# Where the bias of the exponentials is made, and the form of the rotary sums, in a two-layer hybrid attention trunk

## The chip, the cores and the metric

The kernel runs on one core of a Trainium2 chip. A core has TensorE (PE in the profile; PEld is its weight load), VectorE (DVE), ScalarE (ACT), GpSimd (POOL) and SyncE (SP), which here issues all DMAs. The metric is the device time of one execution in microseconds; the time given is the median of several runs.

## The reference

Two decoder layers over 1024 tokens of width 1024. Layer 0 uses mixer A, dilated sliding-window attention with 16 heads of 64 in three groups (window 128 with stride 1, 512 with stride 4, 2048 with stride 16), merged by their softmax denominators. Layer 1 uses mixer B, sliding-window attention (128) with 16 query heads on 2 key heads and one sink logit a head. Queries and keys are rotated; the output is gated by SiLU, projected, normed with a residual, and a second gate adds a projection of p.

```python
def apply_rope(t, cos, sin):
    t1, t2 = tf[..., :half], tf[..., half:]
    return jnp.concatenate([t1 * c - t2 * s, t2 * c + t1 * s], axis=-1)

# banded_attention, for each query over its band of keys
m = jnp.max(s, axis=-1, keepdims=True)
if sinks is not None:
    m = jnp.maximum(m, sk)
e = jnp.exp(s - m)
l = jnp.sum(e, axis=-1, keepdims=True)
if sinks is not None:
    l = l + jnp.exp(sk - m)
o = jnp.einsum('bnhgqk,bnkhd->bnqhgd', e, v) / l
...
for i in range(DEPTH):
    h = mixer(x)                       # A, then B
    x = layer_norm(DEEPNORM_ALPHA * x + h, ln_g[i], ln_b[i])
    x = x + sigmoid(x @ ple_w_gate[i]) * (p[i] @ ple_w_proj[i])
```

## The kernel before, in words

All large products run in float16 with operands split into a high and a low half (three matmuls for one, `lin`, lines 262 to 272). Weights come in blocks of 512 columns: SyncE loads a block, VectorE finds its largest value (line 108), ScalarE writes the high half (131) and VectorE the low half (132). A block's work is cut into eight token tiles of 128.

Layer A goes through two pairs of head quarters and in each through the three groups in the order 1, 2, 0; each group has its own token order (`token_orders`). For a group the values are made first (eight tiles), then two blocks of queries and keys. For each tile of these `rope_out` reads the product from PSUM: two multiplications on VectorE with the cosine and the sine (line 344, tiles t1 and t2), a difference and a sum on GpSimd over the 32-column halves (346, 347), then, one tile later, a split into high and low half (353, 354), a copy with halves exchanged (357) and a DMA transpose to qk (358).

A *unit* is the attention of four heads for one tile of queries: `scores` makes the scores on TensorE (381), masks them and takes the row maxima on VectorE (385), makes the bias nbias of the exponentials from the maxima, the negated scale ncs and a constant on VectorE (387), takes four exponentials on ScalarE (391), splits the result (395 on ScalarE, 397 on GpSimd or VectorE), and transposes it by DMA to pT (400). `pv` multiplies by the values, two units later in layer A and three in layer B. There are 96 units in layer A and 32 in layer B. The nbias columns are kept with the output in tile st in layer A (the merge of the groups reads them) and in tile sb in layer B.

In layer B the bias is also limited by the sinks: `self.nsink`, made once, holds the negated sink plus the constant, and line 389 takes the minimum on VectorE. For every second unit `after` makes the denominators of eight heads: the sum of bias and sinks (842, tile se), its exponential on ScalarE (843), the sum with the row sums (844) and the reciprocal (845). `outp` writes the scaled output to tile mu on VectorE (849).

The tables for rotation, in the three token orders, and the masks lie in one constant tile `tab`, loaded at the start in two pieces (452, 458).

The order of the instructions on each engine is set by the framework's scheduler, which simulates the program with its own costs: the code's order and waits are kept, but instructions of an engine can change places.

Of the kernel before, what the change touches and what calls it, by code (L numbers as in the profile page):

```python
# [10 lines left out]
F32 = mybir.dt.float32  # L11
# [3 lines left out]
AF = mybir.ActivationFunctionType  # L15
ALU = mybir.AluOpType
# [4 lines left out]
P = 128  # L21
S = 1024
D = 1024
NT = S // P
NK = D // P
PLE = 256
HD = 64
# [26 lines left out]
def const_table():  # L54
    inv = np.array(INV_FREQ, np.uint32).view(np.float32)
    ang = np.arange(S, dtype=np.float32)[:, None] * inv[None, :]
    cos = np.cos(ang.astype(np.float64)).astype(np.float32) * np.float32(2.0 ** -QK_SHIFT)
    sin = np.sin(ang.astype(np.float64)).astype(np.float32) * np.float32(2.0 ** -QK_SHIFT)
    rope = []
    for o in token_orders():  # L60
        for t in (cos, sin):
            rope.append(t[o].transpose(1, 0, 2).reshape(P, NT * 32))
    r = np.arange(P)[:, None]
    c = np.arange(P)[None, :]

    def m(keep):
        return np.where(keep, 0.0, NEG).astype(np.float32)

    parts = rope + [
        m(c >= r), m(c <= r),  # L70
        m(c >= r + 1), m(c <= r),
        m((c <= r) & ((c - r) % 2 == 0)),
        np.eye(P, dtype=np.float32),
    ]
    return np.ascontiguousarray(np.concatenate(parts, axis=1))
# [6 lines left out]
N_WAKE = 8  # L82
Z_AHEAD = 3
ROWS_AHEAD = 4
N_ROPE = 6 * NT * 32
N_CONST = N_ROPE + 6 * P


class Block:
# [49 lines left out]
class Trunk:  # L139
    def __init__(self, ctx, tc, a):  # L140
        self.ctx, self.tc, self.nc, self.a = ctx, tc, tc.nc, a
        nc = self.nc
# [25 lines left out]

        tab = self.const.tile([P, N_CONST], F32, name="tab")
        self.tab = tab  # L170
        self.cos, self.sin = [], []
        for o in range(3):
            for i, lst in enumerate((self.cos, self.sin)):
                b = (2 * o + i) * NT * 32
                lst.append(tab[:, b:b + NT * 32].rearrange("p (n c) -> p n c", n=NT))
        b = N_ROPE
        self.mask_a = tab[:, b:b + 2 * P]
        self.mask_b = tab[:, b + 2 * P:b + 4 * P]
        self.mask_2 = tab[:, b + 4 * P:b + 5 * P]
# [10 lines left out]
    def keep(self, cols=1, name="k"):  # L190
        self.uid += 1
        return self.const.tile([P, cols], F32, name=f"{name}{self.uid}", tag=f"{name}{self.uid}")

    def pow2(self, mx, s, inv):

# [134 lines left out]
        self.nc.vector.tensor_scalar(n, c, -1.0, None, op0=ALU.mult)  # L330
        return c, n

    def rope_out(self, ps, nq, nk, order, n, dst):

        nc, w = self.nc, self.work
        nh = nq + nk
        t1 = w.tile([P, 512], F32, tag="t1", name="t1")
        t2 = w.tile([P, 512], F32, tag="t2", name="t2")  # L340
        pv = ps.rearrange("p (h c) -> p h c", c=32)
        for t, tb in ((t1, self.cos[order]), (t2, self.sin[order])):
            tv = t[:, :nh * HD].rearrange("p (h c) -> p h c", c=32)
            nc.vector.tensor_mul(tv, pv, tb[:, n, :].unsqueeze(1).to_broadcast([P, 2 * nh, 32]))  # L344
        v1, v2 = (t[:, :nh * HD].rearrange("p (h b c) -> p h b c", b=2, c=32) for t in (t1, t2))
        nc.gpsimd.tensor_sub(v1[:, :, 0, :], v1[:, :, 0, :], v2[:, :, 1, :])  # L346
        nc.gpsimd.tensor_add(v1[:, :, 1, :], v1[:, :, 1, :], v2[:, :, 0, :])  # L347
        nb = nh + nk
        hl = w.tile([P, 12, P], F16, tag="hl", name="hl", bufs=3)
        rv = t1[:, :nh * HD].rearrange("p (h c) -> p h c", c=HD)  # L350

        def parts():
            nc.scalar.activation(hl[:, :nh, 0:HD], rv, AF.Copy)  # L353
            nc.gpsimd.tensor_sub(hl[:, :nh, HD:P], rv, hl[:, :nh, 0:HD])  # L354
            if nk:
                src, to = (hl[:, a:b, :].rearrange("p h (w c) -> p h w c", w=2) for a, b in ((nq, nh), (nh, nb)))
                nc.vector.tensor_copy(to, src[:, :, ::-1, :])  # L357
            nc.sync.dma_start(dst, hl[:, :nb, :].rearrange("p b c -> p (b c)"), transpose=True)

        self.ends.append(parts)  # L360
# [7 lines left out]
    def scores(self, qa, kas, mask, cs, ncs, sums, nbias, floor, pool_lo):  # L368
# [6 lines left out]
        for pr in range(2):  # L375
# [7 lines left out]
            for i in range(2):  # L383
                h = 2 * pr + i
                nc.vector.tensor_tensor_reduce(sm[:, h, :nk], ps[:, i, :nk], mask, 1.0, -3e38, ALU.add, ALU.max,  # L385
                                               mx[:, h:h + 1])
        nc.vector.tensor_scalar(nbias, mx, ncs, LN_PSCALE, op0=ALU.mult, op1=ALU.add)  # L387
        if floor is not None:
            nc.vector.tensor_tensor(nbias, nbias, floor, op=ALU.min)
        for h in range(4):  # L390
            nc.scalar.activation(sm[:, h, :nk], sm[:, h, :nk], AF.Exp, bias=nbias[:, h:h + 1], scale=cs,  # L391
                                 accum_out=sums[:, h:h + 1])
# [41 lines left out]
    def startup(self):  # L434
# [4 lines left out]
        with tc.tile_pool(name="start", bufs=1) as st:  # L439
# [9 lines left out]
                    nc.sync.dma_start(raw[:, 0, 1024 * kt:1024 * kt + n], a[src][0][:, 1024 * kt:1024 * kt + n])  # L449
            part(pr[:, 0, :], a["pT"][0], 256, 1024)  # L450
            part(wr[:, 0, :], a["wple"][0], 512, 1024)
            nc.sync.dma_start(self.tab[:, N_CONST - P:], a["tab"][:, N_CONST - P:])
            nc.sync.dma_start(pr[:, 1, :], a["pT"][1])
            nc.sync.dma_start(wr[:, 1, :], a["wple"][1])
            for c in range(NK):
                nc.sync.dma_start(xr[:, c, :], a["xT"][:, c, :])
            self.blocks[0].load()
            nc.sync.dma_start(self.tab[:, :N_CONST - P], a["tab"][:, :N_CONST - P])
            nc.sync.dma_start(self.sinks, a["sinks"].partition_broadcast(P))

            idle = st.tile([P, 512], F16, name="idle", tag="pro", bufs=14)
# [158 lines left out]
    def layer_a(self):  # L620
# [13 lines left out]
        cvs = {}  # L634
        for pair in range(2):
            for g in (1, 2, 0):
                blk = self.next_block()
                cvs[pair, g] = self.prod(self.invx, blk.inv, 2.0 ** V_SHIFT, "cv")
                slots = [i for i in range(3) if i != slots[1]]
# [7 lines left out]
                for i in range(2):  # L647
# [4 lines left out]
                    for n in range(NT):  # L652
                        ps = self.ps_lin.tile([P, 512], F32, tag="lin", name="lin")
                        self.lin(ps, blk, *self.stat_a(g, n), 0, 512)
                        qk.append(at.tile([P, 12, P], F16, tag="qk", name="qk", bufs=8))
                        self.rope_out(ps, 4, 4, g, n, qk[n])
                        self.unit_a(2 * pair + i, g, n, qk, v1, v2, cs, ncs,
                                    cvs[pair, g], scr)
                        self.progress()
# [122 lines left out]
    def layer_b(self, xT, invx):  # L782
# [2 lines left out]
        self.z_dr = [self.dram.tile([P, D], F32, name=f"zb{n}", tag=f"zb{n}") for n in range(NT)]  # L785
        self.set_lag(3)
        self.bufs = 3
        self.nsink = self.kv.tile([P, 16], F32, name="nsink", tag="nsink")
        nc.vector.tensor_scalar(self.nsink, self.sinks, -1.0, LN_PSCALE, op0=ALU.mult, op1=ALU.add)
        blk = self.next_block()  # L790
        cv = self.prod(invx, blk.inv, 2.0 ** V_SHIFT, "cv")
        ck = self.prod(invx, blk.inv, 2.0 ** QK_SHIFT, "ck")
# [3 lines left out]
        for n in range(NT):  # L796
            ps = self.ps_lin.tile([P, 512], F32, tag="lin", name="lin")
            self.lin(ps[:, :256], blk, *self.stat_t(xT, n), 0, 256)
            self.v_out(ps[:, P:2 * P].rearrange("p (h c) -> p h c", c=HD), vh[:, n], vl[:, n])
            self.rope_out(ps[:, :P], 0, 2, 0, n, kT[n])  # L800
            self.progress()
        blk.released = True
        self.upt = 1.5
        for kv in range(2):
# [3 lines left out]
            nc.vector.tensor_scalar(cs, cs, 1e-20, None, op0=ALU.max)  # L808
            ncs = self.keep(1, "ncs")
            nc.vector.tensor_scalar(ncs, cs, -1.0, None, op0=ALU.mult)  # L810
            for n in range(NT):
                ps = self.ps_lin.tile([P, 512], F32, tag="lin", name="lin")
                self.lin(ps, blk, *self.stat_t(xT, n), 0, 512)
                qT = at.tile([P, 8, P], F16, tag="qk", name="bq", bufs=9)
                self.rope_out(ps, 8, 0, 0, n, qT)
                tile_st = []
                for hg in range(2):
                    self.unit_b(kv, n, hg, qT, kT, vh, vl, cs, ncs, cv, tile_st)
# [5 lines left out]
    def unit_b(self, kv, n, hg, qT, kT, vh, vl, cs, ncs, cv, tile_st):  # L824
# [22 lines left out]
        def outp(o, r):  # L847
# [4 lines left out]

        self.later(UNIT_LAG, lambda: self.unit(lambda h: qT[:, 4 * hg + h, :], kas, mask, cs, ncs,
                                          lambda h, kb: vh[:, tiles[kb], kv, :], lambda h, kb: vl[:, tiles[kb], kv, :],
                                          stats, outp, hg == 1, self.nsink[:, c0:c0 + 4], after if hg else None))


    def transpose_rows(self, src, s, dst, i, name):
# [276 lines left out]
```

## Time and profile before

| | |
|---|---|
| median of 3 runs | 1719.22 us (1716.74 to 1722.72) |
| profiled execution | 1715.05 us, span 1713.3 us |
| mean granted TensorE clock | 0.980 |
| DMA | 309.06 MB, mean 180 GB/s |

All profile lines come from the one profiled execution. A row of instructions gives line, engine, operation, output<-input by the program's names, shapes and count, then the busy time in us and the mean ns of one, then the idle time of the engine before them and what ended it. A row with three numbers behind a colon, as 215/229/1759, gives the shortest, median and longest duration in ns. In the timeline the columns are start, length, engine, line and operation; the brackets at the end give the idle time before it and what ended it. A matmul's length includes its way through the pipeline, so matmuls that follow each other overlap: rows of 0.38 us start 0.22 us apart.

### The profile page before, as it was taken

Reading aid. Unit: us, or ns where it says so; the run is one execution under the profiler, and the core shown is the slowest. Engines: PE = TensorE matmul, PEld = TensorE weight load, DVE = VectorE, ACT = ScalarE, POOL = GpSimd, SP = SyncE. Lnnn points to the kernel's source line nnn. Section 1 sums busy time; section 2 is a strip of 40 time slices with the busy share of each in tenths; the row PEclk is TensorE's granted clock in tenths of the full one; section 3 lists DMA queues with packets and bytes.
Section 4 is the critical chain, followed back from the end, with each engine's and each line's share of the span. In section 5 each row is a group of like instructions: output and inputs, shape, how many; then the busy total and the mean of one; then the engine's idle time right before and its main releaser. Section 6 shows DMA issues by size and latency. Waiting matters only on the chain. (4 is left out here: it accounts for less than half of the span.)

```text
span 1713.3 us, 29175 instructions
## 1 busy us (share of the span) xinstructions
PE 1595.0 (93%) x10579; PEld 882.3 (51%) x10579; DVE 1163.1 (68%) x2846; ACT 837.6 (49%) x1818; POOL 700.2 (41%) x601
## 2 busy tenths in 40 slices
PE   9899999999998889999999988689999898979998
PEld 3455566654555456666545543234464555534444
DVE  6767656765677776567567776787457988767731
ACT  4425554554654365545545663523334677753221
POOL 1115524532655665155235553443324553123431
PEclk9999999999999999999999999799999999989999
DMA  9618865764778787477558887989965798787963
GB/s 367 225 59 163 161 142 128 161 142 117 154 155 220 184 165 153 112 155 162 120 131 169 182 221 224 297 226 259 251 172 113 143 188 179 170 277 217 239 201 111
DMA packets 542785, 309.06 MB, mean 180 GB/s; under 512 B 473008, under 2 KB 494128, under 8 KB 542256
## 3 DMA queue, kind: packets, MB, share of 16 engines
q1 hardware_dynamic: 542640, 307.20, 73.2%
q8 instruction: 83, 1.36, 0.3%
q14 instruction: 62, 0.51, 0.1%
HBM read 135.82 MB, written 54.92 MB: 111 GB/s over the span
## 5 line engine op out<-in xcount | busy, mean ns | idle before, releaser
L268 PE MATMUL lin<-whl,xhl 128*128 128x512 f16 x1280 | 488.1, 381 | 0.0
L269 PE MATMUL lin<-whl,xhl 128*128 128x512 f16 x1280 | 486.9, 380 | 0.0
L270 PE MATMUL lin<-whl,xhl 128*128 128x512 f16 x1280 | 486.5, 380 | 0.0
L391 ACT ACTIVATE sm<-sm,st,cs 128x128 f32<-128x128 f32 (+1 forms) x384 | 203.6, 531 | 171.1 <-DVE st L387 144.2
L397 POOL TENSOR_TENSOR phl<-sm,phl 128x1024 f16<-128x1024 f32 (+1 forms) x88 | 160.3, 1821 | 257.2 <-ACT phl L395 240.5
L108 DVE TENSOR_REDUCE wpm<-wraw 128x1 f32<-128x1024 f32 (+1 forms) x132 | 156.8, 1197 | 93.2 <-DMA wraw<-in_wa_dram 49.8
L270 PEld LDWEIGHTS <-xhl 128*128 128x128 f16 x1280 | 149.0, 116 | 126.8 <-issue 1.9
L268 PEld LDWEIGHTS <-xhl 128*128 128x128 f16 x1280 | 149.0, 116 | 118.2 <-issue 1.8
L269 PEld LDWEIGHTS <-xhl 128*128 128x128 f16 x1280 | 149.8, 117 | 115.6 <-issue 1.3
L346 POOL TENSOR_TENSOR t<-t,t 128x256 f32<-128x256 f32 (+1 forms) x120 | 93.4, 778 | 275.1 <-DVE t L344 265.3
L354 POOL TENSOR_TENSOR hl<-t,hl 128x512 f16<-128x512 f32 (+1 forms) x120 | 140.2, 1169 | 102.5 <-ACT hl L353 102.5
L385 DVE CUSTOM_DVE_ANT_0 sm<-s,tab 128x256 f32<-128x256 f32 (+1 forms) x512 | 157.2, 358 | 30.8 <-PE s L381 26.5
L344 DVE TENSOR_TENSOR t<-lin,tab 128x512 f32<-128x512 f32 (+1 forms) x240 | 147.6, 654 | 28.0 <-PE lin L270 27.8
L132 DVE SCALAR_TENSOR_TENSOR whl<-wraw,s,whl 128x1024 f16<-128x1024 f32 (+1 forms) x116 | 156.6, 1394 | 3.1 <-ACT whl L131 3.1
L353 ACT ACTIVATE hl<-t 128x512 f16<-128x512 f32 (+1 forms) x120 | 72.3, 603 | 174.8 <-POOL t L347 155.7
L131 ACT ACTIVATE whl<-wraw,s 128x1024 f16<-128x1024 f32 (+1 forms) x116 | 122.0, 1123 | 21.7 <-DVE s L208 14.0
L268 PE MATMUL lin<-whl,x2T 128*128 128x512 f16 (+1 forms) x320 | 116.5, 364 | 0.0
L270 PE MATMUL lin<-whl,x2T 128*128 128x512 f16 (+1 forms) x320 | 116.2, 363 | 0.0
L269 PE MATMUL lin<-whl,x2T 128*128 128x512 f16 (+1 forms) x320 | 116.2, 363 | 0.0
L395 ACT ACTIVATE phl<-sm 128x1024 f16<-128x1024 f32 (+1 forms) x128 | 110.7, 865 | 2.2
L412 PEld LDWEIGHTS <-pT 128*128 128x128 f16 x800 | 72.4, 98 | 51.6 <-DMA pT<-phl 49.3
L357 DVE COPY hl<-hl 128x512 f16<-128x512 f16 (+1 forms) x104 | 50.4, 484 | 71.5 <-POOL hl L354 71.2
(189 smaller groups left out, 2940.1 us busy)
## 6 DMA issues: line engine op xcount, KB each, us to landing
wraw<-in_wa_dram SPq DMA_DIRECT2D x56, 512.0 KB, 5.5
scr<-st SPq DMA_DIRECT2D x96, 132.0 KB, 2.5
gt<-scr SPq DMA_DIRECT2D x48, 264.0 KB, 3.4
wraw<-in_wav_dram SPq DMA_DIRECT2D x24, 512.0 KB, 5.8
prh<-pro SPq DMA_DIRECT2D x32, 256.0 KB, 3.6
wraw<-in_wg_dram SPq DMA_DIRECT2D x16, 512.0 KB, 7.0
wraw<-in_wb_dram SPq DMA_DIRECT2D x16, 512.0 KB, 5.6
xg<-y SPq DMA_DIRECT2D x16, 512.0 KB, 3.8
```

Source lines behind the costliest of these rows:

```text
L108: k.nc.vector.tensor_reduce(pm[:, c:c + 1], self.raw[:, c * q:(c + 1) * q], axis=AX.X, op=ALU.max, apply_absolute_value=True)
L131: nc.scalar.activation(hl[:, 0, sl], self.raw[:, sl], AF.Copy, scale=self.s)
L132: nc.vector.scalar_tensor_tensor(hl[:, 1, sl], self.raw[:, sl], self.s, hl[:, 0, sl], op0=ALU.mult, op1=ALU.subtract)
L268: mm(ps, xh(kt), wh, start=(kt == 0), stop=False)
L269: mm(ps, xh(kt), wl, start=False, stop=False)
L270: mm(ps, xl(kt), wh, start=False, stop=(kt == NK - 1))
L344: nc.vector.tensor_mul(tv, pv, tb[:, n, :].unsqueeze(1).to_broadcast([P, 2 * nh, 32]))
L354: nc.gpsimd.tensor_sub(hl[:, :nh, HD:P], rv, hl[:, :nh, 0:HD])
L385: nc.vector.tensor_tensor_reduce(sm[:, h, :nk], ps[:, i, :nk], mask, 1.0, -3e38, ALU.add, ALU.max, mx[:, h:h + 1])
L391: nc.scalar.activation(sm[:, h, :nk], sm[:, h, :nk], AF.Exp, bias=nbias[:, h:h + 1], scale=cs, accum_out=sums[:, h:h + 1])
L395: nc.scalar.activation(hl[:, 0], sm[:, :, :nk], AF.Copy)
L397: eng.tensor_sub(hl[:, 1], sm[:, :, :nk], hl[:, 0])
```

## The change

Three things change.

The bias. `scores` no longer makes nbias with a VectorE operation; a ScalarE activation (copy, with a scale and a constant) writes it just ahead of the exponentials. The sinks are compared before that: `self.sk_cs` holds the sinks divided by the scale cs (a reciprocal and a product for each of the two key heads), and VectorE takes the maximum of mx and sk_cs.

The rotary sums. The sine table has 64 columns a tile, the first 32 negated. The second product reads PSUM with the two 32-column halves exchanged, so that the rotated value is t1 + t2, one GpSimd addition over 512 columns in place of a subtraction and an addition over 256 each.

The tables. They lie in a tile `rope` with two buffers, loaded by `rope_tables` for each group of layer A (six loads of 384 KB) and once for layer B; `tab` keeps the masks and the identity.

```diff
-        for t in (cos, sin):
-            rope.append(t[o].transpose(1, 0, 2).reshape(P, NT * 32))
+        for t in (cos, np.concatenate([-sin, sin], 1)):
+            rope.append(t[o].transpose(1, 0, 2).reshape(P, -1))
...
+    def rope_tables(self, order):
+        t = self.const.tile([P, N_ROPE], F32, name="rope", tag="rope", bufs=2)
+        self.nc.sync.dma_start(t, self.a["tab"][:, order * N_ROPE:(order + 1) * N_ROPE])
+        self.cos = t[:, :NT * 32].rearrange("p (n c) -> p n c", n=NT)
+        self.sin = t[:, NT * 32:].rearrange("p (n b c) -> p n b c", n=NT, b=2)
...
-        for t, tb in ((t1, self.cos[order]), (t2, self.sin[order])):
-            tv = t[:, :nh * HD].rearrange("p (h c) -> p h c", c=32)
-            nc.vector.tensor_mul(tv, pv, tb[:, n, :].unsqueeze(1).to_broadcast([P, 2 * nh, 32]))
-        v1, v2 = (t[:, :nh * HD].rearrange("p (h b c) -> p h b c", b=2, c=32) for t in (t1, t2))
-        nc.gpsimd.tensor_sub(v1[:, :, 0, :], v1[:, :, 0, :], v2[:, :, 1, :])
-        nc.gpsimd.tensor_add(v1[:, :, 1, :], v1[:, :, 1, :], v2[:, :, 0, :])
+        cos = self.cos[:, n, :].unsqueeze(1).to_broadcast([P, 2 * nh, 32])
+        nc.vector.tensor_mul(t1[:, :nh * HD].rearrange("p (h c) -> p h c", c=32), pv, cos)
+        pb = ps.rearrange("p (h b c) -> p h b c", b=2, c=32)[:, :, ::-1, :]
+        sin = self.sin[:, n].unsqueeze(1).to_broadcast([P, nh, 2, 32])
+        nc.vector.tensor_mul(t2[:, :nh * HD].rearrange("p (h b c) -> p h b c", b=2, c=32), pb, sin)
+        nc.gpsimd.tensor_add(t1[:, :nh * HD], t1[:, :nh * HD], t2[:, :nh * HD])
...
-        nc.vector.tensor_scalar(nbias, mx, ncs, LN_PSCALE, op0=ALU.mult, op1=ALU.add)
         if floor is not None:
-            nc.vector.tensor_tensor(nbias, nbias, floor, op=ALU.min)
+            nc.vector.tensor_max(mx, mx, floor)
+        nc.scalar.activation(nbias, mx, AF.Copy, scale=ncs, bias=LN_PSCALE)
         for h in range(4):
             nc.scalar.activation(sm[:, h, :nk], sm[:, h, :nk], AF.Exp, bias=nbias[:, h:h + 1], scale=cs,
...
-            nc.sync.dma_start(self.tab[:, :N_CONST - P], a["tab"][:, :N_CONST - P])
+            nc.sync.dma_start(self.tab[:, :N_CONST - P], a["tab"][:, 3 * N_ROPE:3 * N_ROPE + N_CONST - P])
...
             for g in (1, 2, 0):
+                self.rope_tables(g)
                 blk = self.next_block()
...
-        self.nsink = self.kv.tile([P, 16], F32, name="nsink", tag="nsink")
-        nc.vector.tensor_scalar(self.nsink, self.sinks, -1.0, LN_PSCALE, op0=ALU.mult, op1=ALU.add)
+        self.rope_tables(0)
+        self.sk_cs = self.kv.tile([P, 16], F32, name="sk_cs", tag="sk_cs")
...
+            rcs = self.keep(1, "rcs")
+            nc.vector.reciprocal(rcs, cs)
+            nc.vector.tensor_scalar(self.sk_cs[:, 8 * kv:8 * kv + 8], self.sinks[:, 8 * kv:8 * kv + 8], rcs, None,
+                                    op0=ALU.mult)
...
-                                          stats, outp, hg == 1, self.nsink[:, c0:c0 + 4], after if hg else None))
+                                          stats, outp, hg == 1, self.sk_cs[:, c0:c0 + 4], after if hg else None))
```

The order of the instructions moves with it. The new lines have other numbers: maxima 387, the bias on ScalarE 391, the maximum with the sinks 390, exponentials 393, copy 359, products 345 and 348, the sum on GpSimd 349, the value matmuls 414 to 416, se<-sb,sinks 849.

*Layer A, the unit whose maxima end at 505.9 us.* VectorE before, from its last maximum (row ISA) on; st<-mx is the bias, whl a weight split, hl the exchanged copy:

```order
L385 ISA sm,mx<-s,tab 128x256
L385 ISA mx 128x1
L357 COPY hl<-hl 128x512
L132 SCALAR_TENSOR_TENSOR whl<-wraw,s_5424,whl 128x1024 x2
L387 TENSOR_SCALAR st<-mx,ncs_4835 128x4
L132 SCALAR_TENSOR_TENSOR whl<-wraw,s_5424,whl 128x1024 x2
L357 COPY hl<-hl 128x512
```

VectorE now at the same place, and behind it ScalarE (hl is a tile's rotary split, vh the values, phl the split of the exponentials sm):

```order
L387 ISA sm,mx<-s,tab 128x256
L387 ISA mx 128x1
L359 COPY hl<-hl 128x512
L132 SCALAR_TENSOR_TENSOR whl<-wraw,s_5383,whl 128x1024 x4
L359 COPY hl<-hl 128x512
L747 TENSOR_REDUCE mM<-gt 128x8
```

```order
L355 ACTIVATE hl<-t_5413 128x8x64
L391 ACTIVATE st<-mx,ncs_4801 128x4
L393 ACTIVATE sm,st<-sm,st,cs_4798 128x256 x4
L366 ACTIVATE vh<-lin 128x2x256
L397 ACTIVATE phl<-sm 128x1024
```

The bias has left VectorE's queue, where it stood behind a copy and two weight splits, and stands on ScalarE between the rotary split and the exponentials.

*Layer B, VectorE, one of the 16 places where se<-sb,sinks reads the bias.* Before (mdt, mde and mdd belong to the scale of a weight block):

```order
L385 ISA mx 128x1
L222 TENSOR_SCALAR mdt<-m_16534 128x1
L387 TENSOR_SCALAR sb<-mx,ncs_13883 128x4
L224 TENSOR_SCALAR mde<-mdt 128x1
L389 TENSOR_TENSOR sb<-sb,nsink 128x4
L226 TENSOR_SCALAR mdd<-tab,mde 128x128
L344 TENSOR_TENSOR t_15147<-lin,tab 128x512
L344 TENSOR_TENSOR t_15148<-lin,tab 128x512
L842 TENSOR_TENSOR se<-sb,sinks 128x8
```

Now:

```order
L387 ISA mx 128x1
L226 TENSOR_SCALAR mde<-mdt 128x1
L852 RECIPROCAL se<-se 128x8
L390 TENSOR_TENSOR mx<-mx,sk_cs 128x4
L228 TENSOR_SCALAR mdd<-tab,mde 128x128
L849 TENSOR_TENSOR se<-sb,sinks 128x8
L345 TENSOR_TENSOR t_15051<-lin,rope 128x512
L348 TENSOR_TENSOR t_15052<-lin,rope 128x512
```

One small operation stands where there were two, and the sum, which now waits for ScalarE's sb, stands ahead of the two rotary products here; over the 16 places, ten have a rotary product, a split or more between the maximum and the sum.

*The start of layer A, TensorE, behind the scores of the fourth unit.* Before:

```order
L381 MATMUL s<-qk 128x128
L268 LDWEIGHTS xhl
L268 MATMUL lin<-whl,xhl 128x512
L269 LDWEIGHTS xhl
L269 MATMUL lin<-whl,xhl 128x512
L270 LDWEIGHTS xhl
L270 MATMUL lin<-whl,xhl 128x512
```

Now:

```order
L383 MATMUL s<-qk 128x128
L270 LDWEIGHTS xhl
L270 MATMUL lin<-whl,xhl 128x512
L271 LDWEIGHTS xhl
L271 MATMUL lin<-whl,xhl 128x512
L414 LDWEIGHTS pT
L414 MATMUL o<-vh,pT 128x64
```

The value matmuls of the second unit (o<-vh,pT) stand 19 matmuls of `lin` earlier than before; those of the third, fourth and fifth unit 8, 32 and 21 earlier. After that TensorE's order differs in small moves only.

More of the change, by code (lines that the diff above doesn't have):

```diff
@@ L84 @@
 ROWS_AHEAD = 4
-N_ROPE = 6 * NT * 32
-N_CONST = N_ROPE + 6 * P
+N_ROPE = 3 * NT * 32
+N_CONST = 6 * P
 class Block:
@@ L170, in __init__ @@
         self.tab = tab
[L171 to L176, printed above, removed]
+        b = 0
         self.mask_a = tab[:, b:b + 2 * P]
@@ L331, in qk_scales, with rope_out @@
         return c, n
-    def rope_out(self, ps, nq, nk, order, n, dst):
+    def rope_out(self, ps, nq, nk, n, dst):
         nc, w = self.nc, self.work
@@ L451, in startup @@
             part(wr[:, 0, :], a["wple"][0], 512, 1024)
-            nc.sync.dma_start(self.tab[:, N_CONST - P:], a["tab"][:, N_CONST - P:])
+            nc.sync.dma_start(self.ident, a["tab"][:, 3 * N_ROPE + N_CONST - P:])
             nc.sync.dma_start(pr[:, 1, :], a["pT"][1])
@@ L655, in layer_a @@
                         qk.append(at.tile([P, 12, P], F16, tag="qk", name="qk", bufs=8))
-                        self.rope_out(ps, 4, 4, g, n, qk[n])
+                        self.rope_out(ps, 4, 4, n, qk[n])
                         self.unit_a(2 * pair + i, g, n, qk, v1, v2, cs, ncs,
@@ L799, in layer_b @@
             self.v_out(ps[:, P:2 * P].rearrange("p (h c) -> p h c", c=HD), vh[:, n], vl[:, n])
-            self.rope_out(ps[:, :P], 0, 2, 0, n, kT[n])
+            self.rope_out(ps[:, :P], 0, 2, n, kT[n])
             self.progress()
@@ L814, in layer_b @@
                 qT = at.tile([P, 8, P], F16, tag="qk", name="bq", bufs=9)
-                self.rope_out(ps, 8, 0, 0, n, qT)
+                self.rope_out(ps, 8, 0, n, qT)
                 tile_st = []
```

## The prediction

> **What bounds the kernel now.** I read the page's busy times first, then a table of stages, then what TensorE waits for, then one unit of attention step by step.
>
> ```profile
> span 1713.3 us, 29175 instructions
> PE 1595.0 (93%) x10579; PEld 882.3 (51%) x10579; DVE 1163.1 (68%) x2846; ACT 837.6 (49%) x1818; POOL 700.2 (41%) x601
> ```
>
> The profiled execution took 1715.05 us, its span is 1713.3 us, and the median of the runs shown is 1719.22 us, 4.2 us more. I sum against 1715.05 and add 4.2 at the end. TensorE is busy for 93% of the span, so at most about 118 us could be won without taking matmuls away, and the change takes none away. The question is which part of TensorE's idle time hangs on what the change touches.
>
> The stages (from the table of windows, columns: stretch, length, then busy time and count of PE, PEld, DVE, ACT, POOL, then the granted clock and DMA): start, layer A, its end with layer norm and gate, layer B, the last end.
>
> ```profile
> 0.00:100.00 100.00, 90.60 (x342) 42.74 (x343) 72.81 (x127) 44.56 (x59) 11.33 (x11) 0.97 0.69 256
> 100.00:1040.00 940.00, 895.92 (x6392) 530.05 (x6391) 630.69 (x1675) 495.33 (x1206) 438.60 (x402) 0.99 0.70 155
> 1040.00:1300.00 260.00, 230.93 (x1145) 112.67 (x1144) 173.28 (x330) 92.15 (x121) 96.82 (x82) 0.95 0.84 232
> 1300.00:1510.00 210.00, 190.13 (x1828) 110.69 (x1826) 175.89 (x514) 141.43 (x355) 81.15 (x62) 0.98 0.79 167
> 1510.00:1713.00 203.00, 187.41 (x879) 86.13 (x877) 110.41 (x201) 64.10 (x77) 72.27 (x46) 0.97 0.73 209
> ```
>
> In layer A TensorE is idle for 44 us and VectorE is 67% busy; in layer B TensorE is idle for 20 us and VectorE is 84% busy. The waits of TensorE say on whom it waits (first two rows: layer A alone; the others: the whole span; columns: total, times, longest):
>
> ```profile
> PE o L412 <- DMA pT<-phl: 36.6, 28, 4.0
> PE s L381 <- DMA qk<-hl: 5.3, 2, 4.7
> ...
> PE o L412 <- DVE mu L849: 14.2, 8, 3.9
> PE lin L268 <- DVE whl L132: 21.7, 1, 21.7
> PE s L233 <- DVE mdd L226: 4.9, 1, 4.9
> ```
>
> The 36.6 us are the value matmuls of layer A that stand before their transposed probabilities have landed. The chain to such a transpose is: scores, four masked maxima on VectorE (line 385), the bias (387), four exponentials on ScalarE (391), the split (395, 397), the DMA. The change acts on the bias. The 21.7 us belong to the end of layer A, where no attention is left to do.
>
> One unit of layer A, followed through VectorE, ScalarE and TensorE:
>
> ```profile
> 505.81 0.09 DVE L385 DVE_READ_ACCUMULATOR2_ANT mx<- 128x1 f32 x1
> 506.67 0.80 DVE L357 COPY hl<-hl 128x512 f16<-128x512 f16 x1 [0.77 <-POOL hl L354]
> 507.39 3.85 DVE L132 SCALAR_TENSOR_TENSOR whl<-wraw,s,whl 128x1024 f16<-128x1024 f32 x2
> 511.17 0.22 DVE L387 TENSOR_SCALAR st<-mx,ncs 128x4 f32<-128x4 f32 x1
> ...
> 508.23 0.62 ACT L353 ACTIVATE hl<-t 128x512 f16<-128x512 f32 x1
> 511.42 0.60 ACT L391 ACTIVATE sm<-sm,st,cs 128x256 f32<-128x256 f32 x1 [2.57 <-DVE st L387]
> ...
> 523.79 0.20 PE L412 MATMUL o<-vh,pT 128*128 128x64 f16 x1 [2.61 <-DMA pT<-phl]
> ```
>
> The maxima are ready at 505.90, but the 0.22 us of bias starts at 511.17: it stands on VectorE behind a copy that waits for GpSimd and behind two weight splits. ScalarE, free at 508.85, waits 2.57 us for it, and 12 us later TensorE waits 2.61 us. So it is the bias's place in VectorE's queue that costs, not its arithmetic.
>
> **The change, part by part.** The prices:
>
> ```profile
> L387 DVE TENSOR_SCALAR st<-mx,ncs 128x4 f32<-128x4 f32 x96 | 40.9, 426 | 1.6
> L387 DVE TENSOR_SCALAR sb<-mx,ncs 128x4 f32<-128x4 f32 x32 | 15.7, 493 | 0.3
> L389 DVE TENSOR_TENSOR sb<-sb,nsink 128x4 f32<-128x4 f32 x32 | 14.5, 454 | 0.2
> L387 DVE TENSOR_SCALAR st<-mx,ncs x96: 215/229/1759, 130.3 to 1016.1; 128x4 f32<-128x4 f32 x96
> L843 ACT ACTIVATE se<-se 128x8 f32<-128x8 f32 x16 | 3.1, 193 | 0.0
> L346 POOL TENSOR_TENSOR t<-t,t 128x256 f32<-128x256 f32 x112 | 89.8, 802 | 266.6 <-DVE t L344 258.4 <-DVE se L842 3.3 <-DVE mde L224 3.0
> L347 POOL TENSOR_TENSOR t<-t,t 128x256 f32<-128x256 f32 x112 | 88.3, 789 | 0.0
> L969 POOL TENSOR_TENSOR xgr<-xgr,prr 128x512 f32<-128x512 f32 x30 | 39.1, 1306 | 92.7 <-DVE prr L968 89.9 <-DVE rr L995 2.8
> L344 DVE TENSOR_TENSOR t<-lin,tab 128x512 f32<-128x512 f32 x224 | 143.8, 681 | 28.0 <-PE lin L270 27.8
> L357 DVE COPY hl<-hl x104: 211/293/2201, 118.6 to 1295.9; 128x512 f16<-128x512 f16 x96, 128x256 f16<-128x256 f16 x8
> ```
>
> *The bias in layer A.* VectorE loses 40.9 us in 96 instructions. ScalarE gains 96 of about 0.2 us (the nearest row, a 128x8 activation, takes 193 ns), 19 us in a stage where it is busy for 495 of 940 us. On the chain it replaces a median of 0.229 us by 0.2 us, which is nothing; what goes is the queue. In the unit shown, ScalarE could begin at 508.85 instead of waiting to 511.17: about 2.2 of the 2.61 us come back. Not every stall is of this kind. In another,
>
> ```profile
> 540.41 0.23 DVE L387 TENSOR_SCALAR st<-mx,ncs 128x4 f32<-128x4 f32 x1
> 540.73 0.60 ACT L391 ACTIVATE sm<-sm,st,cs 128x256 f32<-128x256 f32 x1
> ...
> 544.38 1.27 POOL L758 TENSOR_TENSOR gt<-gt 128x512 f32<-128x512 f32 x1
> 545.61 2.14 POOL L397 TENSOR_TENSOR phl<-sm,phl 128x1024 f16<-128x1024 f32 x1
> ...
> 553.63 0.20 PE L412 MATMUL o<-vh,pT 128*128 128x64 f16 x1 [2.64 <-DMA pT<-phl]
> ```
>
> the exponentials follow the bias at once, and the lateness is GpSimd's, busy with a merge until 545.65; nothing comes back of these 2.64 us. Of the two, 2.2 of 5.25 us return, 42%. Applied to 36.6 us that is 15 us. The ends are 0 (each next wait takes over) and 30 us (all but a few waits go). From the 15 I take 3 us: in the new order the value matmuls of the second to fifth unit stand 8 to 32 matmuls earlier (the rows of TensorE shown with the change), up to 7 us, so that some wait there is new. **Term: -12 us.**
>
> *The bias in layer B.* VectorE loses line 387 (15.7 us) and keeps one small operation with the sinks; the maximum that replaces line 389 has two inputs in SBUF like it, so I price it at the same 454 ns. That is 16 us less in a stage where VectorE has 34 us of slack, and TensorE's 14.2 us of waits for mu are waits for VectorE. Against it stands a new wait: the sum se<-sb,sinks, on VectorE before and after, now reads a bias that ScalarE makes. Behind it on VectorE stand the rotary products and then the maxima of the next unit, for which GpSimd, ScalarE and TensorE wait. How late ScalarE can be:
>
> ```profile
> ACT sm L391 <- DVE sb L389: 39.6, 17, 4.7
> ...
> 1348.11 4.25 ACT L131 ACTIVATE whl<-wraw,s 128x1024 f16<-128x1024 f32 x4
> ```
>
> In 17 of 32 units ScalarE waited for VectorE; in the other 15 it was still busy, for up to the 4.25 us of a weight split. So of 16 sums about half find no bias, by about 2.1 us: 17 us. In 10 of the 16 places the new order puts a rotary product or more between the maximum and the sum (0.68 us each), which covers part; I take 10 us of waits. VectorE's net is 16 - 10 = 6 us, and TensorE's part of it about a third. **Term: -2 us**, ends -17 (all of mu's waits and a little more) and +20.
>
> *The rotary sums.* GpSimd loses two operations of 802 and 789 ns and gets one of 128x512, which as the sum of line 969 takes 1306 ns: 285 ns less for each of 112 tiles, 32 us of GpSimd's 700. On TensorE's path lie only the 5.3 us of waits for qk. The second product reads PSUM with its 32-column halves exchanged; line 357 copies with the same exchange in SBUF at a median of 293 ns for 512 columns, no slower than plain operations of its size in the rows above, so I price the product at the same 681 ns; if it took half as long again, 112 times 0.34 us would be 38 us of VectorE. **Term: -1 us**, ends -5 and +8.
>
> *The tables.* The load at the start shrinks from
>
> ```profile
> tab<-in_tab_dram SPq DMA_DIRECT2D x1, 1088.0 KB, 11.6
> ```
>
> to 320 KB, and seven loads of 384 KB are added. 768 KB at the first stage's 256 GB/s are 3 us of traffic taken from beside the first weights, whose maxima TensorE waits for (4.9 us, line 226); two of the new loads follow behind the first stores. The other five are issued by SyncE a group ahead of their use, between the transposes; each is smaller than a 512 KB weight piece, and there is no wait on another engine in front of it, since its buffer was last read a group before. A transpose that falls behind one may be a us late. **Term: 0**, ends -3 and +5.
>
> Sum: -12 - 2 - 1 + 0 = -15 us: 1700 us against the profiled execution's 1715.05, and 1719.2 - 15 = 1704 us against the median.
>
> [...] Line 387 takes 215 ns at least, 229 in the median and 1759 at worst, while the 128x8 activation hardly spreads around its 193 ns. [...]
>
> **The rivals.**
> - *The stalls only move* (no change). The transposes land earlier, but the next waits, for GpSimd's split and for VectorE's backlog before the maxima, stand behind; the second example speaks for it, the first against. Layer A gives 4 us or less: 1715 to 1723 us.
> - *More comes back.* Each removed queue also lets VectorE start the next maxima earlier, and layer A gives its 30 us; with 2 to 8 of layer B that is 1681 to 1693 us. The 34 us of slack in layer B against 310 in A speak for A alone.
> - *VectorE stands behind ScalarE* (slower). If each of the 16 sums meets a whole weight split on ScalarE, VectorE stands for 16 times 4.25 = 68 us, less the 16 saved; half of its 34 us of slack may take up 17, and 35 us lengthen layer B. With 12 us from layer A that is +23: 1742 us. It decides from a mean wait of (16 + 17 + 12)/16 = 2.8 us on. For it speaks that ScalarE is busy for 141 of 210 us there; against it that in 17 of 32 units ScalarE was the one to wait.
> - *GpSimd's longer hold.* Line 357, at 293 ns in the median and 2201 at worst, shows that VectorE's operations stand for GpSimd's. One sum of 1.3 us holds for 0.65 us on average whoever meets it, against 0.4 us for each of two; with 112 meetings that is 28 us of VectorE, most of its 41 us in layer A, and some 10 of the 12 us there would be gone: 1714 us. [...]
>
> **The numbers.** My forecast, 1694 to 1712 us: 0.60. More comes back: 0.14. Stalls only move: 0.13. GpSimd's hold, at the edge between faster and same: 0.05. VectorE behind ScalarE: 0.08. A difference of 0.3% is 5 us here. So faster is 0.60 + 0.14 + 0.02 = 0.76, same 0.13 + 0.03 = 0.16, slower 0.08. The range reaches from 1687 to 1719: it leaves out the slower case and the better half of the second rival.
>
> **What would show it.** Right: line 391 on ScalarE near 0.2 us and the first exponential right behind it; TensorE's waits for pT in layer A at 20 to 26 us instead of 36.6; VectorE's busy time down by some 50 us, GpSimd's by 30; the second product at 0.68 us. Wrong: a VectorE wait for sb on ScalarE in layer B of over 30 us; products over 0.8 us; waits for pT that stay at 36 us with the maxima later by what the bias gained; new waits for qk where a table load stands before the transpose.

## The result, and the profile after

The changed kernel takes 1693.39 us (median of 4 runs, 1692.93 to 1693.99) against 1719.26 us (1716.74 to 1722.72; four runs, the 1719.22 above is of three): a ratio of 0.9848, 95% interval 0.9831 to 0.9866, so 26 us less (23 to 29). The forecast was 1704 us, 1687 to 1719. The direction and the range were right; the terms for the bias, which make up nearly all of the sum, were not, as the runs below show.

The profiled execution of the changed kernel, its span and busy times, and TensorE's waits in layer A (first two rows) and over the span:

```profile
span 1691.2 us, 29008 instructions
PE 1588.7 (94%) x10579; PEld 880.7 (52%) x10579; DVE 1139.0 (67%) x2721; ACT 873.0 (52%) x1946; POOL 676.7 (40%) x481
```

```profile
PE o L414 <- DMA pT<-phl: 31.4, 21, 3.6
PE s L383 <- DMA qk<-hl: 5.2, 4, 2.2
...
PE lin L270 <- issue: 21.6, 1, 21.6
...
PE o L414 <- DVE mu L856: 5.5, 4, 2.0
```

The waits for pT in layer A went from 36.6 us to 31.4, not to the 20 to 26 forecast; the waits for mu, which are layer B's, from 14.2 to 5.5; the stall behind layer A is unchanged (21.7 and 21.6). The 5 us less for pT are not clear of the spread between executions, as the runs below show. The stages (columns as before; layer A, its end, layer B):

```profile
100.00:1030.00 930.00, 892.85 (x6372) 528.49 (x6371) 612.98 (x1579) 521.18 (x1301) 425.46 (x306) 0.99 0.69 159
1030.00:1287.00 257.00, 230.21 (x1151) 112.44 (x1150) 174.66 (x334) 91.86 (x121) 92.90 (x70) 0.95 0.85 233
1287.00:1489.00 202.00, 188.65 (x1842) 110.89 (x1841) 164.19 (x476) 150.63 (x388) 73.54 (x48) 0.99 0.86 176
```

In layer B TensorE now stands for 13 of 202 us, before for 20 of 210. The prices of the moved and new operations:

```profile
L391 ACT ACTIVATE st<-mx,ncs 128x4 f32<-128x4 f32 x96 | 28.1, 293 | 115.3 <-DVE mx L387 115.1
L391 ACT ACTIVATE sb<-mx,ncs 128x4 f32<-128x4 f32 x32 | 9.3, 292 | 24.4 <-DVE mx L390 24.4
L390 DVE TENSOR_TENSOR mx<-mx,sk_cs 128x4 f32<-128x4 f32 x32 | 9.0, 284 | 0.2
L849 DVE TENSOR_TENSOR se<-sb,sinks 128x8 f32<-128x8 f32 x16 | 4.8, 298 | 1.7 <-ACT sb L391 1.7
L348 DVE TENSOR_TENSOR t<-lin,rope 128x512 f32<-128x512 f32 x112 | 76.1, 680 | 0.0
L349 POOL TENSOR_TENSOR t<-t,t 128x512 f32<-128x512 f32 x112 | 148.1, 1322 | 260.2 <-DVE t L348 231.1 <-DMA scr<-st 10.0 <-DVE mL L754 7.7
L359 DVE COPY hl<-hl 128x512 f16<-128x512 f16 x96 | 53.2, 555 | 80.7 <-POOL hl L356 80.5
```

The bias takes 293 ns on ScalarE, not 0.2 us. The exchanged product takes 680 ns (681 forecast), the one sum 1322 (1306). The new wait in layer B, priced at 10 us, is 1.7 us in all (last column of line 849).

### The profile page after: what moved, and what is told of

The parts are those of the page before. It is cut to its first block, busy times and chain, and to the rows that moved or that the text cites. A ratio compares the mean times of both kernels' runs of the same rounds, so it can differ in the third digit from the quotient of the medians.

```text
span 1691.2 us, 29008 instructions
## 1 busy us (share of the span) xinstructions
PE 1588.7 (94%) x10579; PEld 880.7 (52%) x10579; DVE 1139.0 (67%) x2721; ACT 873.0 (52%) x1946; POOL 676.7 (40%) x481
## 5 line engine op out<-in xcount | busy, mean ns | idle before, releaser
L349 POOL TENSOR_TENSOR t<-t,t 128x512 f32<-128x512 f32 (+1 forms) x120 | 152.7, 1272 | 269.5 <-DVE t L348 238.5
L356 POOL TENSOR_TENSOR hl<-t,hl 128x512 f16<-128x512 f32 (+1 forms) x120 | 144.6, 1205 | 122.9 <-ACT hl L355 122.9
L132 DVE SCALAR_TENSOR_TENSOR whl<-wraw,s,whl 128x1024 f16<-128x1024 f32 (+1 forms) x116 | 164.9, 1475 | 3.5 <-ACT whl L131 3.5
L270 PE MATMUL lin<-whl,x2T 128*128 128x512 f16 (+1 forms) x320 | 115.2, 360 | 0.0
L271 PE MATMUL lin<-whl,x2T 128*128 128x512 f16 (+1 forms) x320 | 115.1, 360 | 0.0
L272 PE MATMUL lin<-whl,x2T 128*128 128x512 f16 (+1 forms) x320 | 115.0, 359 | 0.0
L359 DVE COPY hl<-hl 128x512 f16<-128x512 f16 (+1 forms) x104 | 55.2, 531 | 83.6 <-POOL hl L356 83.4
L345 DVE TENSOR_TENSOR t<-lin,rope 128x512 f32<-128x512 f32 (+1 forms) x120 | 78.8, 657 | 37.9 <-PE lin L272 37.7
```

The lines of the kernel that those rows point to most:

```text
L132: nc.vector.scalar_tensor_tensor(hl[:, 1, sl], self.raw[:, sl], self.s, hl[:, 0, sl], op0=ALU.mult, op1=ALU.subtract)
L270: mm(ps, xh(kt), wh, start=(kt == 0), stop=False)
L271: mm(ps, xh(kt), wl, start=False, stop=False)
L272: mm(ps, xl(kt), wh, start=False, stop=(kt == NK - 1))
L349: nc.gpsimd.tensor_add(t1[:, :nh * HD], t1[:, :nh * HD], t2[:, :nh * HD])
```

## The experiments

All are edits of the changed kernel or of the one before, each timed beside the kernel before on its chip. Differences in us are the ratio less 1, times 1719. The stage lengths are cut at the same projection matmul in each trace: layer A, its end, layer B, the last end; the table is of one profiled execution each.

| kernel | bias A / B made on | time, us | ratio (95%) | us | A | end of A | B | end |
|---|---|---|---|---|---|---|---|---|
| before | VectorE / VectorE | 1719.26 | 1 | 0 | 979.4 | 221.5 | 241.5 | 201.4 |
| changed | ScalarE / ScalarE | 1693.39 | 0.9848 (0.9831 to 0.9866) | -26 | 974.4 | 217.0 | 230.4 | 200.7 |
| bias_only | ScalarE / ScalarE | 1691.85 | 0.9844 (0.9817 to 0.9870) | -27 | 967.5 | 217.4 | 234.8 | 204.5 |
| rope_tables | VectorE / VectorE | 1719.23 | 1.0005 (0.9987 to 1.0023) | +1 | 983.7 | 217.1 | 243.4 | 205.4 |
| tables_only | VectorE / VectorE | 1721.10 | 1.0014 (0.9997 to 1.0031) | +2 | 986.5 | 218.3 | 241.7 | 202.8 |
| bias_a | ScalarE / VectorE | 1712.11 | 0.9967 (0.9953 to 0.9981) | -6 | 980.0 | 217.4 | 242.4 | 204.8 |
| bias_b | VectorE / ScalarE | 1704.86 | 0.9921 (0.9897 to 0.9946) | -14 | 979.0 | 217.9 | 232.6 | 201.8 |
| dve_dummy | ScalarE / ScalarE | 1703.72 | 0.9904 (0.9872 to 0.9936) | -17 | 977.0 | 219.4 | 234.9 | 201.2 |
| dummy_b | ScalarE / ScalarE | 1700.96 | 0.9902 (0.9884 to 0.9920) | -17 | 977.9 | 217.9 | 234.2 | 201.0 |

One profile settles a stage to some 5 us only. In layer A all engines have the same instructions in the same order in the changed kernel, bias_a, dummy_b and fill (a few instructions at the edge of the stage aside); the stage took 974.4, 980.0, 977.9 and 975.2 us. Layer B has one order in the changed kernel, bias_b, dve_dummy and fill, and took 230.4, 232.6, 234.9 and 232.3 us. TensorE's waits for pT in layer A, 31.4 us in the changed kernel, are these in bias_a, dummy_b and fill:

```profile
PE o L416 <- DMA pT<-phl: 35.0, 20, 3.1
PE o L417 <- DMA pT<-phl: 34.7, 20, 4.3
PE o L414 <- DMA pT<-phl: 30.7, 22, 3.3
```

### Which part of the change does it

**bias_only**: the kernel before with the new bias alone, old sums, old tables (the sinks compared as in the change).

```diff
-        nc.vector.tensor_scalar(nbias, mx, ncs, LN_PSCALE, op0=ALU.mult, op1=ALU.add)
         if floor is not None:
-            nc.vector.tensor_tensor(nbias, nbias, floor, op=ALU.min)
+            nc.vector.tensor_max(mx, mx, floor)
+        nc.scalar.activation(nbias, mx, AF.Copy, scale=ncs, bias=LN_PSCALE)
```

> The kernel before with the bias on ScalarE and the maximum with the sinks, rotary sums and tables as before. Queue theory (the gain comes from the bias leaving VectorE's queue, which shortens the way from the maxima to pT and to mu): 1693 to 1701 us, VectorE about 45 us less busy. Rotary theory (half the gain is GpSimd's shorter sum): 1704 to 1710 us.

**rope_tables**: the changed kernel with this edit undone. **tables_only**: the kernel before with the tables loaded for each token order, nothing else.

> The changed kernel with the bias back on VectorE (lines 387 and 389 of before). Queue theory: 1712 to 1720 us, GpSimd about 30 us less busy than before and TensorE's waits for pT and mu as before. Rotary theory: 1702 to 1710 us.

> The kernel before with nothing but the tables loaded per token order (cosine and unsigned sine, 256 KB a load). Both theories: 1716 to 1722 us. If the lighter start gave part of the gain: 1713 us or less, with the first block of layer A some 3 us earlier. If loads between the transposes cost: 1722 us or more and waits for qk of over 8 us.

The bias alone gives 27 us, the other two parts together nothing (+1, interval -2 to +4), the tables nothing (+2, -1 to +5). So the whole gain is the bias's, as far as these runs can tell. bias_only came out 1 us below its range and rope_tables within its own; the loads were off: VectorE is 28 us less busy in bias_only, not 45, and GpSimd 19 us less in rope_tables, not 30.

### Which layer

**bias_a** and **bias_b**: the changed kernel with ScalarE's bias in one layer only, `if floor is None` choosing layer A.

> The changed kernel with ScalarE's bias in layer A only; layer B has the two VectorE operations of before. If layer A gives the 9 to 12 us that the stage lengths show (changed rotary sums with and without the bias: 983.7 and 974.4 us; the old sums with and without: 979.4 and 967.5 us) and layer B its own part, the time is 1706 to 1711 us. If the prediction's sizes hold (12 in A, 2 in B), 1706 to 1708. If nearly all of the gain is layer B's, 1714 to 1719 us.

> The changed kernel with ScalarE's bias (and the one maximum with the sinks) in layer B only; layer A has VectorE's bias of before. By the stage lengths layer B gives 7 to 13 us: 1706 to 1712 us. If the prediction's size for layer B holds (2 us), 1716 to 1718 us. With bias_a the two gains should add up to the whole 26 us within 5.

Layer A alone gives 6 us (3 to 8), layer B alone 14 us (9 to 18). bias_a missed its range by 1 us upwards, bias_b by 1 us downwards. The 2 us forecast for B are refuted. The 12 of A are not settled: alone it gives half of them, but where layer B has ScalarE's bias already (bias_b against the changed kernel, each by its ratio) it gives 12 us (7 to 18). The two alone add up to 19 against 26; the expectation allowed 5 for that, and the 7 left are open (the three intervals together are about 6 us wide to each side). The stages say the same of B: it takes 241.5 to 243.4 us in the four kernels with VectorE's bias there, 230.4 to 234.9 in the five with ScalarE's. Of bias_b's 14 us, 9 to 11 lie in this stage. In layer A the two groups nearly touch: 979.0 to 986.5 us with VectorE's bias, 967.5 to 980.0 with ScalarE's. TensorE's waits for mu, of bias_a and of bias_b:

```profile
PE o L416 <- DVE mu L855: 16.4, 11, 3.8
```

```profile
PE o L416 <- DVE mu L858: 6.3, 5, 2.1
```

### Queue or load

**dve_dummy**: the changed kernel, and in layer A VectorE also writes the old product to a spare place that nobody reads; **dummy_b** the same in layer B (`floor is not None`, into a tile md).

```diff
         nc.scalar.activation(nbias, mx, AF.Copy, scale=ncs, bias=LN_PSCALE)
+        if floor is None:
+            nc.vector.tensor_scalar(self.spare, mx, ncs, LN_PSCALE, op0=ALU.mult, op1=ALU.add)
```

> The changed kernel, and for each unit of layer A VectorE also does the old bias operation into a column of st that nobody reads, so VectorE's load and order are as before and only the chain is the new one. If the gain in layer A is the chain's: within 3 us of the changed kernel, 1691 to 1697 us. If it is VectorE's lighter load (41 us of busy time): layer A loses its 6 us again, 1699 us or more.

> The changed kernel, and VectorE in layer B also computes the old product (line 387) into a spare tile that nobody reads: VectorE's load there is that of before, the exponentials do not wait for it. If layer B gained because the exponentials no longer stand behind VectorE's queue, it stays within 5 us of the changed kernel: 1692 to 1698 us. If it gained because VectorE has less to do there (it was busy 84% of the stage), most of the 8 to 11 us go: 1700 to 1706 us.

dve_dummy lost about 10 us, outside what the queue alone allows; but only 2.6 of them lie in layer A, where the dummy is, less than the 5.6 us by which executions of one order differ there. The others lie in the end of layer A (2.4; VectorE's order came out otherwise there) and in layer B (4.5), in which no unused operation stands and where all engines have the order of the changed kernel. In the trace of that layer the clock was halved three times, against once (granted clock from 1287 to 1500 us 0.98, in the changed kernel 0.99). It therefore doesn't tell queue from load.

dummy_b gives 17 us where the changed kernel gives 26. In its layer B, 234.2 us, most of the gain against 241.5 is still there, though VectorE is as busy in the layer as before (197.5 us; before 195.7, changed 185.4). Its wait for mu lies between:

```profile
PE o L417 <- DVE mu L859: 11.3, 7, 4.2
```

VectorE's spare operations take this time there:

```profile
L394 DVE TENSOR_SCALAR md<-mx,ncs 128x4 f32<-128x4 f32 x32 | 16.6, 521 | 0.4
```

The 234.2 us lie within the 230.4 to 234.9 of the kernels that have no such operation in the layer, and 7 us below the shortest stage with VectorE's bias. So, by the stage, about two thirds of the gain in B or more come without any relief of VectorE: the exponentials no longer stand behind its queue. How much the load adds is open. That it counts is what the waits for mu say: 11.3 us against 2.8 to 8.0 in the eight other kernels with ScalarE's bias in layer B. And the time is 9 us longer, but the stages place only 3.8 us of that in layer B and 3.5 in layer A, where instructions and order are the changed kernel's. Both expectations missed a part: the time is in the load's range, the stage nearer to the queue's.

### A better pace, or not

**upt70**, **upt77**, **upt80**: the pace of attention units in layer A (`self.upt`, 0.75) changed, to give the transposes more room or to have fewer units left over.

> The changed kernel with the planner's pace of attention units in layer A at 0.70 units for each projection tile in place of 0.75, so that more matmuls of projection stand between the scores and the value matmuls. If what is left of the waits for pT (31.4 us in layer A) is lateness of a few us against a fixed distance, 5 to 12 us go: 1681 to 1689 us. If the waits are set by bursts on GpSimd and on the queue, or if the units that are put off come out at the end of the layer, 1692 to 1702 us.

> The changed kernel with a pace of 0.80 attention units for each projection tile in layer A in place of 0.75. At 0.70 the matmuls of layer A came out 7 us later and the stage behind it 13 us longer, because units were left over at the layer's end. If the leftover is what the pace decides, 0.80 leaves fewer: the stage behind layer A, with its one stall of 21.6 us, gets shorter and the time is 1678 to 1690 us. If the value matmuls then stand too close to their scores, the waits for pT (31.4 us in layer A) grow by 10 us or more: 1697 to 1715 us.

> The same with 0.77, a smaller step: 1685 to 1692 us if the leftover decides, 1694 to 1702 us if the waits for pT grow.

Measured: 1717.37 us (ratio 0.9999, 0.9985 to 1.0014), 1705.85 (0.9940, 0.9920 to 0.9960), 1697.35 (0.9890, 0.9870 to 0.9911): 0.70 loses the whole gain and lies above both of its ranges; 0.80 and 0.77 lie in those for growing waits. At 0.70 the last units come later (72 matmuls of `lin` of layer A stand behind the last value matmul, in the changed kernel 149), and a wait of 31.6 us stands at the end of layer A in place of 21.6:

```profile
PE s L235 <- DVE mdd L228: 38.6, 3, 31.6
```

At 0.77 the waits for pT in layer A did not grow (31.2 us), and at 0.80 they fell, against the expectation:

```profile
PE o L414 <- DMA pT<-phl: 27.4, 16, 4.2
PE s L383 <- DMA qk<-hl: 10.7, 6, 5.7
```

and yet layer A took 984.0 us, 9.6 more; the waits for qk took 5.5 of it, and the clock was halved seven times there in place of five (in the mean over the profiled execution it was 0.975, in the changed kernel's 0.982). What took the rest isn't settled. No pace tried beats the changed kernel, and bias_only can't be told from it.

### The clock

**fill**: the changed kernel with 92 unread matmuls in the stall behind layer A.

```diff
+                if l == 0 and n == 0 and hf == 0:
+                    pf = self.ps_s.tile([P, 512], F32, tag="s", name="s")
+                    fill = self.ones.unsqueeze(1).to_broadcast([P, 4, P])
+                    for i in range(92):
+                        nc.tensor.matmul(pf.rearrange("p (a b) -> p a b", a=4), self.ones, fill, start=(i == 0), stop=(i == 91))
                 self.lin(ps, w_o[hf], *self.stat_t(ogT, n), 0, 512)
```

> The changed kernel, with 92 matmuls of ones by ones (each 512 columns, some 20 us together) that nobody reads, put on TensorE between the last projection of layer A and the first output projection, where TensorE stands idle for 21.6 us and the granted clock is 0.5 for 23.9 us, of which 4.4 us lie behind the stall. If it is TensorE's own idleness that halves the clock, the clock stays at 1.0 there, the first output projections follow at 0.216 us in place of 0.427 us, and the stage is 2.2 us shorter: 1690 to 1693 us. If the clock falls for another reason, the half-clock stretch stays where it is, the fillers take twice as long, and the stage becomes up to 20 us longer: 1695 to 1713 us.

TensorE's rows at that place, of the changed kernel and of fill:

```profile
1059.19 0.38 PE L272 MATMUL lin<-whl,xhl 128*128 128x512 f16 x1
1081.18 0.58 PE L270 MATMUL lin<-whl,ogT 128*128 128x512 f16 x1 [21.61 <-issue]
1081.56 0.63 PE L271 MATMUL lin<-whl,ogT 128*128 128x512 f16 x1
1081.99 0.63 PE L272 MATMUL lin<-whl,ogT 128*128 128x512 f16 x1
```

```profile
1059.73 20.02 PE L918 MATMUL s<-ones 128*128 128x512 bf16 x92
1083.39 0.38 PE L270 MATMUL lin<-whl,ogT 128*128 128x512 f16 x1 [3.64 <-issue]
1083.60 0.38 PE L271 MATMUL lin<-whl,ogT 128*128 128x512 f16 x1
1083.82 0.38 PE L272 MATMUL lin<-whl,ogT 128*128 128x512 f16 x1
```

and the stretch from 1060 to 1085 us in both (the third number from the right is the granted clock):

```profile
1060.00:1085.00 25.00, 3.82 (x10) 1.33 (x11) 18.71 (x38) 13.68 (x19) 12.12 (x8) 0.53 1.03 370
```

```profile
1060.00:1085.00 25.00, 21.36 (x100) 9.58 (x99) 17.53 (x31) 12.51 (x19) 12.37 (x8) 1.00 1.07 359
```

With the fillers the clock stays at 1.0 and the projections behind them start 0.21 us apart, not 0.43, as expected, and the first tile of them (24 matmuls) takes 2.2 us less. So it is TensorE's idleness that halved its clock here. The time missed its range all the same: 1705.74 us (ratio 0.9930, 0.9909 to 0.9951), 12 us above the changed kernel. The stall ended 1.9 us later, and the stage behind it, 228.9 us long against 217.0, has new waits of 2 to 3 us for VectorE and for a transpose; beside the stall they are 15.9 us in sum, against 5.2. Which of the moved instructions causes these was not tried.

## Why the prediction was right or wrong

**The sum.** -15 us forecast, -26 measured: outside the 1694 to 1712 us of the forecast itself by less than 1 us, inside the wider range. B's term was too small by 12 us or more; A's was too large by 6 if the layer is changed alone, and of the right size if it is changed after B. That the range held is in part luck, since neither term came about as forecast.

**Layer A, -12: 6 alone, 12 after B.** The mechanism was seen: the wait for VectorE's bias is gone where VectorE's queue was the cause. The step that failed is "42% of 36.6 us", taken from two stalls. In the profile of the changed kernel these two gave back 2.5 of 5.25 us (2.61 to 1.70 and 2.64 to 1.03), near the 2.2 forecast but not as forecast: the second, put at nothing, gave most. In bias_a, dummy_b and fill, with the same order in layer A, the first is 2.9 to 3.1 us and the second 0.9 to 1.3; in the four kernels with VectorE's bias there they are 2.6 to 4.2 and 2.3 to 2.7. So the second did shrink; that the first did, from which the 42% came, isn't shown. The first, after (VectorE, ScalarE, GpSimd, TensorE; same unit as in the prediction):

```profile
503.59 3.22 ACT L131 ACTIVATE whl<-wraw,s 128x1024 f16<-128x1024 f32 x3
504.35 0.08 DVE L387 DVE_READ_ACCUMULATOR2_ANT mx<- 128x1 f32 x1
...
507.07 0.61 ACT L355 ACTIVATE hl<-t 128x512 f16<-128x512 f32 x1
507.59 0.28 ACT L391 ACTIVATE st<-mx,ncs 128x4 f32<-128x4 f32 x1
507.91 0.60 ACT L393 ACTIVATE sm<-sm,st,cs 128x256 f32<-128x256 f32 x1
...
511.87 2.67 POOL L399 TENSOR_TENSOR phl<-sm,phl 128x1024 f16<-128x1024 f32 x1 [2.79 <-ACT phl L397]
...
521.41 0.20 PE L414 MATMUL o<-vh,pT 128*128 128x64 f16 x1 [1.70 <-DMA pT<-phl]
```

The bias no longer stands behind VectorE's weight splits; it stands behind ScalarE's. The maxima are ready at 504.43, the bias starts at 507.59: 3.16 us against 5.27. The prediction let ScalarE begin as soon as VectorE had done, and forgot that ScalarE too keeps its order. Other stalls grew: one that was 1.78 us at 613.42 is now 2.98 us (2.9 to 3.1 in bias_a, dummy_b and fill; none in rope_tables and bias_b, which have the new sums and VectorE's bias in layer A). The split of the probabilities has come to stand on ScalarE behind a split of rotated values that waits for GpSimd's rotary sum:

```profile
600.28 0.18 ACT L393 ACTIVATION_READ_ACCUMULATOR sm<-sm,st,cs 128x1 f32 x1
600.96 1.65 POOL L349 TENSOR_TENSOR t<-t,t 128x512 f32<-128x512 f32 x1 [1.43 <-DVE t L348]
602.64 0.63 ACT L355 ACTIVATE hl<-t 128x512 f16<-128x512 f32 x1 [2.17 <-POOL t L349]
603.18 1.04 ACT L397 ACTIVATE phl<-sm 128x1024 f16<-128x1024 f32 x1
```

ScalarE's two longest waits from 100 to 1030 us, before and after:

```profile
ACT sm L391 <- DVE st L387: 144.2, 66, 6.8
ACT hl L353 <- POOL t L347: 126.8, 44, 7.5
```

```profile
ACT hl L355 <- POOL t L349: 155.3, 56, 7.4
ACT st L391 <- DVE mx L387: 115.1, 51, 5.8
```

It waits 29.1 us less for VectorE's bias and 28.5 us more for GpSimd. With the bias alone (bias_only) it is 30.6 less and 19.4 more, with the new sums and tables but VectorE's bias (rope_tables) 8.7 less and 7.6 more. Other waits moved too; all of ScalarE's idle time there fell by 32 us, from 433.6 to 401.6, about the 28.1 us that the new instruction takes. By the 6 us that the layer gives alone the rival "the stalls only move" (4 us or less from layer A) was nearer than the forecast, by the 12 us after B it was not.

**Layer B, -2: far too small (-14 alone, -20 after A).** Two steps failed. The new wait of the sums for ScalarE, 10 us, is 1.7 us in five places: "about half find no bias, by 2.1 us" carried over how ScalarE stood under the old order. And "TensorE's part of it about a third" took VectorE's net gain as the only way, where the chain itself was shortened: ScalarE's wait for the bias fell from 39.6 us to 24.4, and TensorE's for mu by 8.7. With fewer long stalls TensorE's clock was halved once in the layer and not three times, worth up to 2 x 1.7 us (an estimate, half of two stretches of 3.41 us; in layer A it was halved five times and not three). The upper end (-17) had been in the text; the term should have lain near it.

**Rotary sums, -1, and tables, 0: right by the time** (+1 for both, +2 for the tables alone, within the measurement). The prices of the product and of the sum were right. GpSimd's work in the rotary sums fell by 30 us, and none of it can be seen in the time.

**The price of the bias.** The nearest row, 193 ns for a 128x8 exponential, was the wrong neighbour: it has neither a scale from SBUF nor a constant. What such a scale comes to stood in other rows of before: line 484 takes 596 ns for 128x512 without one and 686 ns with one (pro<-lin and pro<-lin,cpl, nine each). By an estimate from these rows that is 193 + 90 = 283 ns, near the 293 measured. The bias did lose its spread: 280 to 300 ns in layer A, on VectorE 215 to 1759. ScalarE's busy time rose by 35 us, which the time doesn't show.

**The marks.** VectorE's busy time fell by 24 us and not 50, though 62 us of operations left it (71.1 of lines 387 and 389 before, 9.0 of line 390 after): others became longer, by 38 us in all, such as the copy of line 359, 507 to 555 ns in the mean. In bias_only, where GpSimd's sums are the old ones, it is 33 us already; in rope_tables, with the new sums and VectorE's bias, VectorE's busy time rose by 9.7 us. That copies on VectorE stand for GpSimd the profile of before shows: of the 104 of line 357, the 55 that met no GpSimd instruction took 298 ns at most, and the 28 longer than 440 ns each ended 0.15 us after one that had begun before them (the longest, 2.20 us from 487.37, beside line 397's 2.12 us from 487.30). But the rival on GpSimd's hold comes to some 10 us of VectorE at most and not 28, without a cost that the time shows. Why the others became longer when the small operations left was not tried. "VectorE behind ScalarE" did not come: 1.7 us. "More comes back" gave a time close to the one measured, but by 30 us from layer A, which gave 6 to 12.

## What to carry to other kernels

An operation moved off a queue joins another one: follow the same unit through the queue that receives it, and count what stands ahead of it there, before taking any of the old wait as won. Two stalls read closely are not a share of 28; sum the waits of the engine in the middle, which shows whether they vanish or change their name. Before a few us are read out of one profile's stage, look how much the stage differs between kernels that have the same order there: here 5 us. Where an engine is busy for 84% of a stage, look for the cost in both its load and its queue, and price a new wait with the order that the change makes, not with the old one.

## What was not expected of the hardware

TensorE's granted clock fell to 0.5 after short stalls, in stretches of 3.41 us or a multiple: of the 20 in the profiles of before and changed (two more are cut off by the end of the trace) 14 lasted 3.41 us, two 6.83, two 10.24, one 20.48 and one 23.89. The page's mean of 0.98 hides it. Before, in layer B:

```profile
1304.39 0.38 PE L269 MATMUL lin<-whl,x2T 128*128 128x512 f16 x1
1307.74 1.58 PE L381 MATMUL s<-bk,bq 128*128 128x128 f16 x16 [2.11 <-DMA bq<-hl]
1309.11 0.63 PE L268 MATMUL lin<-whl,x2T 128*128 128x512 f16 x1
1309.54 0.63 PE L269 MATMUL lin<-whl,x2T 128*128 128x512 f16 x1
```

A stall of 2.11 us, and the projections behind it start 0.43 us apart, before it 0.22; the granted clock is 0.51 from 1308.0 to 1311.4 us, 1.00 from 1300 to 1307 and from 1312 to 1316. Of all idle times of TensorE from 66 us on that began at full clock, in 13 profiles (before, changed and the eleven experiments), none of 243 between 0.8 and 2 us was followed by a half clock, 46 of 102 between 2 and 3 us, 30 of 44 between 3 and 4, and all 45 above; in before and changed alone these are none of 40, 8 of 17, all 4 and all 6. By an estimate, half its length, a stretch of 3.41 us costs up to 1.7 us of matmuls, nearly as much as the 2.11 us of the stall that set it off: going by these counts, a stall brought below 2 us saves twice where it had halved the clock.
